# A two-block transformer on one core: row sums from natural-layout rows in the first stage, held order of its loads and splits, padding at the far end of SBUF

## The chip, the core and the metric

The kernel runs on one core of a Trainium2 chip. TensorE (PE) multiplies, VectorE (DVE) and ScalarE (ACT) work element by element, GpSimd (POOL) too, and SyncE (SP) issues the DMAs. All work from SBUF, 128 partitions wide; matmuls end in PSUM, which is used here as eight banks of 128x512 float32. The time is that of the whole program on the device, in microseconds, as the median of several runs. Three runs of the kernel before gave 1665.96, 1666.15 and 1666.22; the median is **1666.15 us**.

## The reference, cut to what matters

Two transformer blocks run one after the other on 512 tokens of 1024 features, float32 throughout. The change touches only how the first things of the first block are computed:

```
mem_n = mem * rsqrt(mean(mem*mem) + 1e-6) * g_mem       # 256 memory tokens
h     = x   * rsqrt(mean(x*x)     + 1e-6) * g_mix       # 512 tokens
k_m, v_m = split(mem_n @ w_mem_kv)                      # 1024 -> 2 x 512
q_m      = h @ w_in[:, 3072:3584]                       # 1024 -> 512
k = rmsnorm(k_m, per head of 128);  q = rmsnorm(q_m, per head of 128)
y_mem = softmax(q k^T / sqrt(128)) v                    # 4 heads
...   # moba attention, short convolution, gates, three branches, w_o, a feed-forward net
...   # second block: pooling branch, spatial gating branch, feed-forward net, gated embedding
```

The factor `rsqrt(mean)` is one number per token. So the kernel multiplies the weights with `mem * g_mem` and `x * g_mix`, not yet divided by the norm, and brings the factor in behind the product, where tokens are rows.

## The kernel before, in words

**Precision and weights.** Each float32 operand is split into a high part, rounded to the matmul's input type by ACT (`AF.Copy`), and a low part, what is left, by DVE (`split`, lines 183 to 190). A product is three matmuls: high by high, high by low, low by high. All weights come as one stream of 288 chunks of 128x1024 (512 KB), in the order in which they are used. Class `Weights` loads a chunk through SP (`load`, line 72), and splits it (`make`: ACT at line 92 writes `whi`, DVE at line 93 writes `wlo`). Raw, high and low chunks have three buffers each. `take` (line 97), called when the first piece of chunk c is used, loads up to chunk c+2 and splits up to chunk c+1. A load waits until the raw buffer is free, that is until the split of the chunk three before it is done; a copy to `whi` waits until TensorE is done with the chunk three before it.

**The first stage.** Nine matmuls on zeros run first (line 153). Then comes the projection of the memory to keys and values (lines 305 to 326), here called kv: eight steps k of 128 features each. A step splits the transposed memory's slice k (`mg{k}`), takes two pieces of 512 columns (one chunk), and does twelve matmuls into four banks `pk`. The memory comes transposed (`memT`, 128x8x256). Its squares are taken by ACT, summed over k by DVE (`Norm.add`, lines 263 to 278), and `per_token` (lines 280 to 288) transposes the sums on TensorE, adds them up on DVE and takes the inverse root (`rsqrt`, lines 239 to 255: ten dependent operations on DVE) to get `rmem`. The tokens come transposed as `xs` (128x8x512) in four loads placed in steps 1 to 4; each slice is split to `h{k}` (lines 341 to 344), and `xn` has its squares and its sum made by POOL (lines 338, 339, 345 and 346).

The keys are copied out of PSUM with the factor `rmem`, normed per head (`normed_rows`, lines 349 to 370) and transposed to `kmT`; the values become `vm`. The queries of the memory heads, here called qm, are 96 matmuls in `gemm_n_steps` (lines 211 to 221): eight steps k, each with four token tiles and three matmuls, two steps to a chunk. `FILL` says how many of these pieces come before the transposes of the keys and before `per_token` of `xn`, which gives `rx`. Then follow the other projections and attention.

**What sets the order.** The program is written in Python; a planner then orders the instructions of each engine by priority and by what its model of costs says is ready, keeps the dependences, and puts in the semaphores. So the order on a queue may differ from the order in the code. SP's queue works in order: a load that waits for a buffer holds up every load behind it.

**Where tiles lie.** Pools are stacked from both ends of SBUF. On the left are the constants, the weights, the operands `h`, the temporaries and most stages. Pools with `side="right"` are stacked from the far end, behind the pool "edge", a spacer of 96 bytes per partition: the memory attention's tiles, `y_conv`, `y_moba`, the pooled branch (`ypool`, `z`, `zs`, `pd`), the gated branch (`ysgu`) and `pT`. `space` (line 120) makes such spacers; others stand in the constants and in the small tiles.

Of the kernel before, what the change touches and what calls it, by code (L numbers as in the profile page):

```python
# [1 line left out]

# [17 lines left out]
KT = 8  # L20
# [6 lines left out]

WARM = 9

FILL = (9, 14, 8)  # L30

ORDER = (2, 3, 1, 0)

# [74 lines left out]
def build(ctx: ExitStack, tc: tile.TileContext, a: dict, out: bass.AP, dbg=None):  # L108
    nc = tc.nc
    mm = nc.tensor.matmul  # L110

    def pool(name, bufs=1, side=None, stack=None, space=None):
        kw = {} if space is None else {"space": space}
        if space is None:
            kw["reuse_waits"] = "tile"
            if side:
                kw["side"] = side
        return (stack or ctx).enter_context(tc.tile_pool(name=name, bufs=bufs, **kw))

# [6 lines left out]
    hpool = pool("operand")  # L126
    tmp = pool("tmp")
    small = pool("small", bufs=2)
    space(small, 64, "s")
    space(pool("edge", side="right"), 96, "e")  # L130
    PS = bass.MemoryType.PSUM
    acc = pool("acc", 5, space=PS)
    ps_s = pool("ps_s", 1, space=PS)
    ps_t = pool("ps_t", 1, space=PS)
    ps_o = pool("ps_o", 1, space=PS)
    W = Weights(nc, wpool, a["weights"])

    def dump(name, ap):
        if dbg is not None and name in dbg:
# [4 lines left out]
    r2 = ExitStack()  # L144
    st = pool("start", stack=r2)


    warm = st.tile([P, 512], BF16, name="warm")
    nc.vector.memset(warm, 0.0)
    nc.scalar.activation(st.tile([P, 1], BF16, name="table"), warm[:, :1], AF.Copy)  # L150
    wps = ps_o.tile([P, 512], F32, tag="po", name="warm")
    for _ in range(WARM):
        mm(wps, lhsT=warm[:, :P], rhs=warm, start=True, stop=True)
    vec = const.tile([P, NV], F32, name="vec")
    nc.sync.dma_start(vec[:, :16], a["vectors"][:, :16])
# [27 lines left out]
    def split(hi, lo, src, scale=None):  # L183

        if scale is None:
            nc.scalar.activation(hi, src, AF.Copy)
            nc.vector.tensor_tensor(lo, src, hi.bitcast(F32), ALU.subtract)
        else:
            nc.scalar.activation(hi, src, AF.Copy, scale=scale)
            nc.vector.scalar_tensor_tensor(lo, src, scale, hi.bitcast(F32), op0=ALU.mult, op1=ALU.subtract)  # L190
# [66 lines left out]
    class Norm:  # L257
# [5 lines left out]
        def add(self, x, by_pool=False):  # L263
            n = self.n

            def square(sq):
                if by_pool:
                    nc.gpsimd.tensor_tensor(sq, x, x, ALU.mult)
                else:
                    nc.scalar.activation(sq, x, AF.Square)  # L270

            if self.sum is None:
                self.sum = tmp.tile([P, 512], F32, tag="nsum", name=self.name + "s", bufs=1)[:, :n]
                square(self.sum)
            else:
                sq = temp(n, self.name + "q")
                square(sq)
                self.engine.tensor_tensor(self.sum, self.sum, sq, ALU.add)
# [23 lines left out]
    yp = pool("memat", stack=r1, side="right")  # L302


    pk = [bank() for _ in range(4)]
    mn = Norm("mem", M)
    for k in range(KT):
        ah, al = pair(st, f"mg{k}", f"mg{k}", 1, M)
        split(ah, al, memT[:, k, :], V("g_mem", k))
        if k == 0:  # L310
            W.make(1, 2)
        ws = [W.take("w_mem_kv", k * P, 512 * x, 512) for x in range(2)]
        mn.add(memT[:, k, :])
        if k == 1:
            nc.sync.dma_start(vec[:, 16:], a["vectors"][:, 16:])
        if 1 <= k < 5:
            q = 2 * k - 2
            nc.sync.dma_start(xs[:, q:q + 2, :], a["xT"][:, q:q + 2, :])
        for x in range(2):
            wh, wl = ws[x]  # L320
            for i in range(2):
                t = slice(i * P, (i + 1) * P)
                d = pk[2 * x + i]
                mm(d, lhsT=ah[:, t], rhs=wh, start=(k == 0), stop=False)
                mm(d, lhsT=al[:, t], rhs=wh, start=False, stop=False)
                mm(d, lhsT=ah[:, t], rhs=wl, start=False, stop=(k == KT - 1))

    qg = const.tile([P, 2], F32, name="qg")
    space(const, 1120, "c")
    nc.vector.tensor_scalar(qg[:, 0:1], V("moba_q_gain"), 64 ** -0.5, None, ALU.mult)  # L330
    nc.vector.tensor_scalar(qg[:, 1:2], V("memq_gain"), 128 ** -0.5, None, ALU.mult)
    rmem = mn.per_token()


    def operand(k):
        return pair(hpool, f"h{k}", f"h{k}", 1)
# [12 lines left out]
    def normed_rows(ps_list, nh, name, scales=None):  # L349
# [22 lines left out]
    vm = [pair(yp, f"vm{i}", f"vm{i}", 1) for i in range(2)]  # L372
    for i in range(2):
        split(*vm[i], pk[2 + i], rmem[:, i:i + 1])
    km_raw = [yp.tile([P, 512], F32, tag=f"kmr{i}", name=f"kmr{i}") for i in range(2)]
    normed_rows([(km_raw[i], pk[i]) for i in range(2)], 4, "km", rmem)
    pq = [bank() for _ in range(4)]
    qm_steps = gemm_n_steps(pq, h, "w_in", 3072)
    for _ in range(FILL[0]):
        next(qm_steps)  # L380
    kmT = [pair(yp, f"kmT{i}", f"kmT{i}", 1, 2 * M) for i in range(2)]
    for g in range(2):
        pt = bank(ps_t, "pt", "kmt")
        for hh in range(2):
# [12 lines left out]

# [577 lines left out]
```

## Time and profile before

| | |
|---|---|
| median of three runs | 1666.15 us |
| profiled execution: its own time | 1665.62 us |
| span of its instructions | 1663.9 us |
| granted TensorE clock, mean | 0.996 |
| TensorE busy | 1641.3 us (99%) |
| DVE, ACT, POOL busy | 956.5, 646.0 and 49.6 us |
| DMA | 161.37 MB, mean 97 GB/s |

The profile is of one execution, and its rows are measured from its first instruction. A row of the timeline has the start in us, the duration in us, the engine, the line, the operation, the output and inputs by name, and in square brackets how long the engine had been idle before it and what ended that. Matmuls are pipelined: two may overlap in such rows, so the distance between starts tells the pace. "PEld" is the loading of the stationary operand, which overlaps with matmuls. A row of groups gives the count, the sum and the mean in ns. A row of stretches gives for each engine the busy time and the count, then the granted clock (1.00 is full speed), the DMA engines' mean busy share and GB/s.

### The profile page before, as it was taken

Reading aid. Unit: us, or ns where it says so; the run is one execution under the profiler, and the core shown is the slowest. Engines: PE = TensorE matmul, PEld = TensorE weight load, DVE = VectorE, ACT = ScalarE, POOL = GpSimd, SP = SyncE. Lnnn points to the kernel's source line nnn. Section 1 sums busy time; section 2 is a strip of 40 time slices with the busy share of each in tenths; the row PEclk is TensorE's granted clock in tenths of the full one; section 3 lists DMA queues with packets and bytes.
Section 4 is the critical chain, followed back from the end, with each engine's and each line's share of the span. In section 5 each row is a group of like instructions: output and inputs, shape, how many; then the busy total and the mean of one; then the engine's idle time right before and its main releaser. Section 6 shows DMA issues by size and latency. Waiting matters only on the chain.

```text
span 1663.9 us, 18992 instructions
## 1 busy us (share of the span) xinstructions
PE 1641.3 (99%) x7553; PEld 1352.5 (81%) x7553; DVE 956.5 (57%) x1382; ACT 646.0 (39%) x927; POOL 49.6 (3%) x54
## 2 busy tenths in 40 slices
PE   6999999999999999999999999999999999999997
PEld 4788777888888888888888888888888888888887
DVE  8667776444556556563332943554467777753355
ACT  5455555222334333332224332333345444432253
POOL 5000000000000000000000300000000000000001
PEclk9999999999999999999999999999999999999999
DMA  5322222234232332323332333222333323323221
GB/s 208 114 77 76 65 62 65 89 101 147 94 101 89 102 100 91 102 92 99 101 117 90 98 102 98 92 89 89 101 102 101 98 93 101 95 95 102 92 99 51
DMA packets 46537, 161.37 MB, mean 97 GB/s; under 512 B 5232, under 2 KB 6640, under 8 KB 46448
## 3 DMA queue, kind: packets, MB, share of 16 engines
q1 hardware_dynamic: 46448, 160.16, 30.2%
q8 instruction: 59, 0.97, 0.2%
q14 instruction: 30, 0.25, 0.0%
HBM read 158.04 MB, written 2.10 MB: 96 GB/s over the span
## 4 chain that ended last, share of the span: by engine, by line
PE 96%; DVE 2%; ACT 1%; issue 0%; DMA 0%; SPq 0%; DVEq 0%; ACTq 0%
PE acc L206 27%; PE acc L207 27%; PE acc L208 27%; PE acc L218 2%; PE acc L220 2%; PE acc L219 2%; PE acc L857 1%; PE acc L856 1%; PE acc L855 1%; PE pat L544 1%; PE sg L791 0%; PE oa L559 0%; PE oa L560 0%; DMA memT<-in_memT 0%; DVE wlo L93 0%
## 5 line engine op out<-in xcount | busy, mean ns | idle before, releaser
L92 ACT ACTIVATE whi<-wraw 128x1024 fp32r<-128x1024 f32 (+1 forms) x289 | 305.5, 1057 | 586.1 <-PE acc L207 363.8
L93 DVE TENSOR_TENSOR wlo<-wraw,whi 128x1024 fp32r<-128x1024 f32 (+1 forms) x289 | 353.9, 1225 | 213.1 <-ACT whi L92 211.9
L206 PE MATMUL acc<-h0h,whi 128*128 128x512 f32 x156 | 62.2, 399 | 0.0
L206 PE MATMUL acc<-h7h,whi 128*128 128x512 f32 x156 | 61.3, 393 | 0.0
L207 PE MATMUL acc<-h0l,whi 128*128 128x512 f32 x156 | 61.2, 392 | 0.0
L206 PE MATMUL acc<-h2h,whi 128*128 128x512 f32 x156 | 61.1, 392 | 0.0
L206 PE MATMUL acc<-h6h,whi 128*128 128x512 f32 x156 | 61.1, 392 | 0.0
L206 PE MATMUL acc<-h5h,whi 128*128 128x512 f32 x156 | 61.1, 391 | 0.0
L206 PE MATMUL acc<-h1h,whi 128*128 128x512 f32 x156 | 61.0, 391 | 0.0
L206 PE MATMUL acc<-h3h,whi 128*128 128x512 f32 x156 | 61.0, 391 | 0.0
L208 PE MATMUL acc<-h0h,wlo 128*128 128x512 f32 x156 | 61.0, 391 | 0.0
L206 PE MATMUL acc<-h4h,whi 128*128 128x512 f32 x156 | 61.0, 391 | 0.0
L208 PE MATMUL acc<-h2h,wlo 128*128 128x512 f32 x156 | 60.9, 390 | 0.0
L208 PE MATMUL acc<-h5h,wlo 128*128 128x512 f32 x156 | 60.9, 390 | 0.0
L207 PE MATMUL acc<-h2l,whi 128*128 128x512 f32 x156 | 60.9, 390 | 0.0
L207 PE MATMUL acc<-h7l,whi 128*128 128x512 f32 x156 | 60.9, 390 | 0.0
L207 PE MATMUL acc<-h5l,whi 128*128 128x512 f32 x156 | 60.9, 390 | 0.0
L207 PE MATMUL acc<-h4l,whi 128*128 128x512 f32 x156 | 60.9, 390 | 0.0
L207 PE MATMUL acc<-h1l,whi 128*128 128x512 f32 x156 | 60.8, 390 | 0.0
L208 PE MATMUL acc<-h6h,wlo 128*128 128x512 f32 x156 | 60.8, 390 | 0.0
L207 PE MATMUL acc<-h6l,whi 128*128 128x512 f32 x156 | 60.8, 390 | 0.0
L208 PE MATMUL acc<-h7h,wlo 128*128 128x512 f32 x156 | 60.8, 390 | 0.0
(1271 smaller groups left out, 4079.8 us busy)
## 6 DMA issues: line engine op xcount, KB each, us to landing
wraw<-in_weights SPq DMA_DIRECT2D x287, 512.0 KB, 3.5
xs<-in_xT SPq DMA_DIRECT2D x4, 512.0 KB, 6.4
x<-in_xT SPq DMA_DIRECT2D x8, 256.0 KB, 5.9
out<-o SPq DMA_DIRECT2D x8, 256.0 KB, 2.1
wraw<-in_weights SPq DMA_DIRECT2D x2, 256.0 KB, 2.8
memT<-in_memT SPq DMA_DIRECT2D x1, 512.0 KB, 6.8
bb<-in_b_spatial SPq DMA_DIRECT2D x1, 512.0 KB, 4.8
ws<-in_w_spatialT SPq DMA_DIRECT2D x1, 512.0 KB, 5.6
```

Of the source, the lines that this page charges most:

```text
L92: nc.scalar.activation(hi[:, s], raw[:, s], AF.Copy)
L93: nc.vector.tensor_tensor(lo[:, s], raw[:, s], hi[:, s].bitcast(F32), ALU.subtract)
L206: mm(ps, lhsT=wh, rhs=ah, start=(k == 0), stop=False)
L207: mm(ps, lhsT=wh, rhs=al, start=False, stop=False)
L208: mm(ps, lhsT=wl, rhs=ah, start=False, stop=(k == n - 1))
L218: mm(ps, lhsT=ah[:, t], rhs=wh, start=(k == 0), stop=False)
L219: mm(ps, lhsT=ah[:, t], rhs=wl, start=False, stop=False)
L220: mm(ps, lhsT=al[:, t], rhs=wh, start=False, stop=(k == n - 1))
L544: nc.tensor.transpose(pt[:, i * P:(i + 1) * P], probs[s_][i][:, c0:c0 + P], ident)
L855: mm(pg, lhsT=wh, rhs=ah[:, t], start=(k == 0), stop=False)
L856: mm(pg, lhsT=wh, rhs=al[:, t], start=False, stop=False)
L857: mm(pg, lhsT=wl, rhs=ah[:, t], start=False, stop=(k == KT - 1))
```

## The change

The sums of squares of the memory and of the tokens are no longer made from the transposed slices. Both tensors are also given in natural layout (`"mem"`, `"x"`: tokens as rows), loaded in tiles of 128 rows of 4 KB (`load_rows`), and ACT squares each tile in place and sums along the row in the same instruction (`row_sums`). The result has one number per token at once, without sums over k, transposes and a reduction. POOL and DVE no longer take part in these sums.

A context manager `as_written` adds an order between successive instructions of SP, ACT and DVE, so that from the first instruction to the last x split the planner keeps the order of the code. That order is written out: the memory's first half goes through ACT's DMA queue, in two loads; the splits of the memory run two steps ahead of their use; x loads, row loads, x splits and row sums each have a step. The kv accumulators use two of the five `acc` banks and the banks `ps_s` and `ps_o`, so that three `acc` banks are free when qm begins. The transposed memory is now in two tiles of 4 KB per partition which share four buffers with the row tiles.

The spacer "edge" has 224 bytes instead of 96, a spacer of 128 bytes is added in the pooled branch's pool behind `ypool`, and the tile "table" in the first stage's pool has 256 bytes instead of 2.

```diff
-FILL = (9, 14, 8)
+FILL = (3, 8)
...
-    space(pool("edge", side="right"), 96, "e")
+    space(pool("edge", side="right"), 224, "e")
...
+    @contextmanager
+    def as_written(*engines):
+        traced = nc.cur_bb.bb.instructions
+        n = len(traced)
+        yield
+        last = {}
+        for i in traced[n:]:
+            if i.engine in engines:
+                if i.engine in last:
+                    tc.add_manual_dep(i, last[i.engine].name, mybir.DependencyInfo(
+                        mybir.DependencyClass.NoSync, mybir.DependencyReason.DATA), reason="order")
+                last[i.engine] = i
...
+    order = as_written(mybir.EngineType.SP, mybir.EngineType.Activation, mybir.EngineType.DVE)
+    order.__enter__()
...
-    nc.scalar.activation(st.tile([P, 1], BF16, name="table"), warm[:, :1], AF.Copy)
...
+    memT = [st.tile([P, D], F32, tag="rows", name=f"memT{i}", bufs=4).rearrange("p (k m) -> p k m", m=M) for i in range(2)]
+    nc.scalar.dma_start(memT[0][:, 0:1, :], a["memT"][:, 0:1, :])
+    nc.scalar.dma_start(memT[0][:, 1:4, :], a["memT"][:, 1:4, :])
+    nc.scalar.activation(st.tile([P, P], BF16, name="table")[:, :1], warm[:, :1], AF.Copy)
     nc.sync.dma_start(vec[:, :16], a["vectors"][:, :16])
-    memT = st.tile([P, KT, M], F32, name="memT")
-    nc.sync.dma_start(memT[:, 0:1, :], a["memT"][:, 0:1, :])
     W.load(1, 2)
-    nc.sync.dma_start(memT[:, 1:2, :], a["memT"][:, 1:2, :])
     W.load(2)
-    nc.sync.dma_start(memT[:, 2:4, :], a["memT"][:, 2:4, :])
-    nc.sync.dma_start(memT[:, 4:8, :], a["memT"][:, 4:8, :])
+    nc.sync.dma_start(memT[1], a["memT"][:, 4:8, :])
     W.load(3)
...
+    def load_rows(name, i):
+        t = st.tile([P, D], F32, tag="rows", name=f"{name}{i}", bufs=4)
+        nc.sync.dma_start(t, a[name][i * P:(i + 1) * P, :])
+        rows.append(t)
+
+    def row_sums(sums, i):
+        t = rows.pop(0)
+        nc.scalar.activation(t, t, AF.Square, accum_out=sums[:, i:i + 1])
...
-    pk = [bank() for _ in range(4)]
-    mn = Norm("mem", M)
+    pk = [bank(), bank(), bank(ps_s, "ps"), bank(ps_o, "po")]
+    ssm = small.tile([P, 4], F32, tag="nss", name="ssm")
+    ssx = small.tile([P, 4], F32, tag="nss", name="ssx")
...
+    make_mg(0)
+    W.make(1, 2)
+    make_mg(1)
     for k in range(KT):
...
         ws = [W.take("w_mem_kv", k * P, 512 * x, 512) for x in range(2)]
-        mn.add(memT[:, k, :])
+        make_mg(k + 2)
         if k == 1:
+            load_x(0)
+        elif k == 3:
+            load_rows("mem", 0)
+        elif k == 4:
+            load_rows("mem", 1)
+        elif k == 5:
+            make_h(0)
+        elif k == 6:
+            load_x(2)
+            row_sums(ssm, 0)
+            make_h(1)
+        elif k == 7:
+            row_sums(ssm, 1)
+            rmem = rsqrt(ssm[:, :2], 2, 1.0 / D, "n")
             nc.sync.dma_start(vec[:, 16:], a["vectors"][:, 16:])
-        if 1 <= k < 5:
-            q = 2 * k - 2
-            nc.sync.dma_start(xs[:, q:q + 2, :], a["xT"][:, q:q + 2, :])
+            load_x(4)
+            load_x(6)
+            make_h(2)
...
-    rmem = mn.per_token()
...
-    xn.engine = nc.gpsimd
-    h = []
-    for k in range(KT):
-        hk = operand(k)
-        split(*hk, xs[:, k, :], V("g_mix", k))
-        h.append(hk)
-    for k in range(KT):
-        xn.add(xs[:, k, :], by_pool=True)
...
-    for _ in range(FILL[0]):
-        next(qm_steps)
...
-    for _ in range(FILL[1]):
-        next(qm_steps)
-    rx = xn.per_token()
+    for k in range(KT):
+        if k == FILL[0]:
+            transpose_km()
+        if k >= 4:
+            row_sums(ssx, k - 4)
+        for _ in range(4):
+            next(qm_steps)
+        if k == 0:
+            for i in range(2):
+                split(*vm[i], pk[2 + i], rmem[:, i:i + 1])
+        elif k == 1:
+            for i in range(2):
+                load_rows("x", i)
+        elif k == 2:
+            for i in range(2, 4):
+                load_rows("x", i)
+        if k + 3 < KT:
+            make_h(k + 3)
+    order.__exit__(None, None, None)
     run(qm_steps)
+    xn.r = rx = rsqrt(ssx, 4, 1.0 / D, "n")
...
     PAD = 32
+    space(pp, 128, "p")
...
+        "x": np.ascontiguousarray(g["x"][0]),
+        "mem": np.ascontiguousarray(g["mem"][0]),
```

More of the change, by code (lines that the diff above doesn't have):

```diff
@@ L1 @@
-from contextlib import ExitStack
+from contextlib import ExitStack, contextmanager
 import concourse.bass as bass
@@ L154, in build @@
     vec = const.tile([P, NV], F32, name="vec")
+    memT = [st.tile([P, D], F32, tag="rows", name=f"memT{i}", bufs=4).rearrange("p (k m) -> p k m", m=M) for i in range(2)]
+    nc.scalar.dma_start(memT[0][:, 0:1, :], a["memT"][:, 0:1, :])
+    nc.scalar.dma_start(memT[0][:, 1:4, :], a["memT"][:, 1:4, :])
+    nc.scalar.activation(st.tile([P, P], BF16, name="table")[:, :1], warm[:, :1], AF.Copy)
     nc.sync.dma_start(vec[:, :16], a["vectors"][:, :16])
-    memT = st.tile([P, KT, M], F32, name="memT")
-    nc.sync.dma_start(memT[:, 0:1, :], a["memT"][:, 0:1, :])
     W.load(1, 2)
-    nc.sync.dma_start(memT[:, 1:2, :], a["memT"][:, 1:2, :])
     W.load(2)
-    nc.sync.dma_start(memT[:, 2:4, :], a["memT"][:, 2:4, :])
-    nc.sync.dma_start(memT[:, 4:8, :], a["memT"][:, 4:8, :])
+    nc.sync.dma_start(memT[1], a["memT"][:, 4:8, :])
     W.load(3)
     xs = st.tile([P, KT, S], F32, name="xs")
+    rows = []
+    def load_rows(name, i):
[5 more added lines that the diff above has]
+        nc.scalar.activation(t, t, AF.Square, accum_out=sums[:, i:i + 1])
     def V(name, j=0):
@@ L261, in __init__, with add @@
             self.name, self.n, self.sum, self.engine = name, n, None, nc.vector
-        def add(self, x, by_pool=False):
+        def add(self, x):
             n = self.n
             def square(sq):
[L267 to L270, printed above, removed]
+                nc.scalar.activation(sq, x, AF.Square)
             if self.sum is None:
@@ L302, in build, with operand, make_h, load_x @@
     yp = pool("memat", stack=r1, side="right")
-    pk = [bank() for _ in range(4)]
-    mn = Norm("mem", M)
+    def operand(k):
+        return pair(hpool, f"h{k}", f"h{k}", 1)
+    h = [operand(k) for k in range(KT)]
+    def make_h(k):
+        split(*h[k], xs[:, k, :], V("g_mix", k))
+    def load_x(k):
+        nc.sync.dma_start(xs[:, k:k + 2, :], a["xT"][:, k:k + 2, :])
+    pk = [bank(), bank(), bank(ps_s, "ps"), bank(ps_o, "po")]
+    ssm = small.tile([P, 4], F32, tag="nss", name="ssm")
+    ssx = small.tile([P, 4], F32, tag="nss", name="ssx")
+    mg = [pair(st, f"mg{k}", f"mg{k}", 1, M) for k in range(KT)]
+    def make_mg(k):
+        if k < KT:
+            split(*mg[k], memT[k // 4][:, k % 4, :], V("g_mem", k))
+    make_mg(0)
+    W.make(1, 2)
+    make_mg(1)
     for k in range(KT):
[L308 to L311, printed above, removed]
+        ah, al = mg[k]
         ws = [W.take("w_mem_kv", k * P, 512 * x, 512) for x in range(2)]
-        mn.add(memT[:, k, :])
+        make_mg(k + 2)
         if k == 1:
+            load_x(0)
[12 more added lines that the diff above has]
+            rmem = rsqrt(ssm[:, :2], 2, 1.0 / D, "n")
             nc.sync.dma_start(vec[:, 16:], a["vectors"][:, 16:])
-        if 1 <= k < 5:
-            q = 2 * k - 2
-            nc.sync.dma_start(xs[:, q:q + 2, :], a["xT"][:, q:q + 2, :])
+            load_x(4)
+            load_x(6)
+            make_h(2)
         for x in range(2):
@@ L329, in build @@
     space(const, 1120, "c")
-    nc.vector.tensor_scalar(qg[:, 0:1], V("moba_q_gain"), 64 ** -0.5, None, ALU.mult)
-    nc.vector.tensor_scalar(qg[:, 1:2], V("memq_gain"), 128 ** -0.5, None, ALU.mult)
-    rmem = mn.per_token()
-    def operand(k):
-        return pair(hpool, f"h{k}", f"h{k}", 1)
-    xn = Norm("x")
-    xn.engine = nc.gpsimd
-    h = []
-    for k in range(KT):
-        hk = operand(k)
-        split(*hk, xs[:, k, :], V("g_mix", k))
-        h.append(hk)
-    for k in range(KT):
-        xn.add(xs[:, k, :], by_pool=True)
+    xn = Norm("x")
     def normed_rows(ps_list, nh, name, scales=None):
@@ L370, in normed_rows, with transpose_km @@
         return raws
-    vm = [pair(yp, f"vm{i}", f"vm{i}", 1) for i in range(2)]
-    for i in range(2):
-        split(*vm[i], pk[2 + i], rmem[:, i:i + 1])
     km_raw = [yp.tile([P, 512], F32, tag=f"kmr{i}", name=f"kmr{i}") for i in range(2)]
     normed_rows([(km_raw[i], pk[i]) for i in range(2)], 4, "km", rmem)
+    vm = [pair(yp, f"vm{i}", f"vm{i}", 1) for i in range(2)]
+    nc.vector.tensor_scalar(qg[:, 0:1], V("moba_q_gain"), 64 ** -0.5, None, ALU.mult)
+    nc.vector.tensor_scalar(qg[:, 1:2], V("memq_gain"), 128 ** -0.5, None, ALU.mult)
+    kmT = [pair(yp, f"kmT{i}", f"kmT{i}", 1, 2 * M) for i in range(2)]
+    def transpose_km():
+        for g in range(2):
+            pt = bank(ps_t, "pt", "kmt")
+            for hh in range(2):
+                for i in range(2):
+                    c = (2 * g + hh) * P
+                    nc.tensor.transpose(pt[:, hh * M + i * P: hh * M + (i + 1) * P], km_raw[i][:, c:c + P], ident)
+            split(*kmT[g], pt, V("memk_gain"))
     pq = [bank() for _ in range(4)]
     qm_steps = gemm_n_steps(pq, h, "w_in", 3072)
-    for _ in range(FILL[0]):
-        next(qm_steps)
[L381 to L384, printed above, removed]
-            for i in range(2):
-                c = (2 * g + hh) * P
-                nc.tensor.transpose(pt[:, hh * M + i * P: hh * M + (i + 1) * P], km_raw[i][:, c:c + P], ident)
-        split(*kmT[g], pt, V("memk_gain"))
-    for _ in range(FILL[1]):
-        next(qm_steps)
-    rx = xn.per_token()
+    for k in range(KT):
[6 more added lines that the diff above has]
+        if k == 0:
+            for i in range(2):
+                split(*vm[i], pk[2 + i], rmem[:, i:i + 1])
[8 more added lines that the diff above has]
+    order.__exit__(None, None, None)
     run(qm_steps)
+    xn.r = rx = rsqrt(ssx, 4, 1.0 / D, "n")
     qm_raw = [yp.tile([P, 512], F32, tag=f"qmr{i}", name=f"qmr{i}") for i in range(4)]
@@ L466, in build @@
     filler = qkv_steps()
-    for _ in range(FILL[2]):
+    for _ in range(FILL[1]):
         next(filler)
```

## The prediction, made before the result

> **What bounds the kernel now.** I read the page's busy times first, then who waits on TensorE, then busy time by stretch, then the order of instructions in the first 70 us.
>
> ```profile
> PE 1641.3 (99%) x7553; PEld 1352.5 (81%) x7553; DVE 956.5 (57%) x1382; ACT 646.0 (39%) x927; POOL 49.6 (3%) x54
> PE 96%; DVE 2%; ACT 1%; issue 0%; DMA 0%; SPq 0%; DVEq 0%; ACTq 0%
> ```
> ```profile
> PE acc L326 <- DVE wlo L93: 8.2, 3, 3.7
> PE acc L324 <- ACT whi L92: 3.2, 3, 1.4
> ```
> TensorE carries the span, and nearly all that it waits for is in two groups of lines 324 to 326, the projection of the memory tokens at the very start (I call it kv; it has eight steps of twelve matmuls). The stretches confirm it:
>
> ```profile
> 5.00:24.00 19.00, 15.10 (x60) 11.02 (x61) 16.71 (x28) 15.73 (x28) 3.78 (x3) 1.00 0.93 338
> 24.00:32.20 8.20, 4.66 (x22) 3.41 (x19) 8.17 (x9) 3.45 (x4) 7.58 (x6) 0.94 0.37 117
> 32.20:45.00 12.80, 9.12 (x21) 6.66 (x22) 12.09 (x13) 2.04 (x4) 11.74 (x11) 0.64 0.27 86
> 400.00:800.00 400.00, 400.00 (x1768) 330.69 (x1767) 221.85 (x280) 146.65 (x180) 0.00 (x0) 1.00 0.30 97
> ```
> The columns are PE, its weight loads, DVE, ACT and POOL, then clock, DMA share and GB/s. From 24 to 45 us DVE and POOL are busy all the time, ACT is nearly idle and DMA is at a third; then the clock falls to 0.64. Later TensorE has no gap at all. So the first 45 us can give, and elsewhere only the pace of the matmuls. The starts of matmuls that mark the steps:
>
> ```profile
> 5.17 0.50 PE L324 MATMUL acc<-whi,mg0h 128*128 128x512 f32 x1 [0.48 <-ACT whi L92]
> 9.54 0.50 PE L324 MATMUL acc<-whi,mg1h 128*128 128x512 f32 x1 [1.30 <-ACT whi L92]
> 13.98 0.50 PE L324 MATMUL acc<-whi,mg2h 128*128 128x512 f32 x1 [1.37 <-ACT whi L92]
> 22.34 0.74 PE L326 MATMUL acc<-wlo,mg4h 128*128 128x512 f32 x2 [1.00 <-DVE wlo L93]
> 24.53 0.39 PE L325 MATMUL acc<-whi,mg5l 128*128 128x512 f32 x1
> 27.09 0.40 PE L324 MATMUL acc<-whi,mg6h 128*128 128x512 f32 x1
> 32.23 1.65 PE L326 MATMUL acc<-wlo,mg6h 128*128 128x512 f32 x3 [3.57 <-DVE wlo L93]
> 34.10 0.63 PE L325 MATMUL acc<-whi,mg6l 128*128 128x512 f32 x1
> 34.53 0.63 PE L326 MATMUL acc<-wlo,mg6h 128*128 128x512 f32 x1
> 41.37 1.55 PE L326 MATMUL acc<-wlo,mg7h 128*128 128x512 f32 x3 [3.65 <-DVE wlo L93]
> 43.99 0.63 PE L218 MATMUL acc<-whi,h0h 128*128 128x512 f32 x1
> 67.96 0.39 PE L218 MATMUL acc<-whi,h0h 128*128 128x512 f32 x1
> ```
> Undisturbed, eleven matmuls take 27.09 - 24.53 = 2.56 us, 0.2325 us each, so a step takes 2.79 us. At the halved clock each takes 0.43 us. From the third step (13.98) to the end of kv (43.99) pass 30.0 us for 72 matmuls that need 72 x 0.2325 = 16.7. The excess of 13.3 us is the waits of 1.00, 3.57 and 3.65, some 18 matmuls at the low clock (18 x 0.195 = 3.5 us), two transposes and short gaps. The second projection (qm, 96 matmuls) runs from 43.99 to 67.96.
>
> **Why DVE is late.** Groups by line and shape in the first 70 us, then one tile's POOL group:
>
> ```profile
> L93 DVE TENSOR_TENSOR wlo<-wraw,whi 128x1024 fp32r<-128x1024 f32 x13 | 16.5, 1272 | 2.5 <-ACT whi L92 2.5
> L190 DVE SCALAR_TENSOR_TENSOR h5l<-xs,vec,h5h 128x512 fp32r<-128x512 f32 x1 | 1.9, 1857 | 0.0
> L190 DVE SCALAR_TENSOR_TENSOR h6l<-xs,vec,h6h 128x512 fp32r<-128x512 f32 x1 | 0.7, 739 | 0.0
> L248 DVE SCALAR_TENSOR_TENSOR nb<-nb,nv 128x2 f32<-128x2 f32 x1 | 1.2, 1230 | 0.0
> L248 DVE SCALAR_TENSOR_TENSOR nb<-nb,nv 128x4 f32<-128x4 f32 x1 | 0.2, 166 | 0.0
> ```
> ```profile
> L278 POOL TENSOR_TENSOR xs<-xs,xq x7: 1262/1738/2213, 27.1 to 40.2; 128x512 f32<-128x512 f32 x7
> ```
> The same ten-operation inverse root takes 0.17 us an operation when POOL is idle and about 1.2 us beside POOL's adds; a split takes 0.74 against 1.86 us. It and the x splits stand ahead of the weight splits that TensorE waits for.
>
> **The change, part by part.** *Removed:* POOL's eight squares and seven adds, ACT's eight squares and DVE's seven adds over the transposed memory rows, six transposes and two reductions. With POOL silent, DVE's operations go back to 0.17 and 0.74 us.
>
> *Added:* six row loads of 512 KB (3.1 MB) and six ACT squares over 128x1024 with an accumulated sum. The trace has no such square; the nearest rows are
>
> ```profile
> 8.43 1.06 ACT L92 ACTIVATE whi<-wraw 128x1024 fp32r<-128x1024 f32 x1 [0.43 <-DMA wraw<-in_weights]
> 12.88 1.04 ACT L92 ACTIVATE whi<-wraw 128x1024 fp32r<-128x1024 f32 x1
> ```
> ```profile
> L724 ACT ACTIVATE vq<-sv x8: 626/628/641, 891.2 to 912.1; 128x512 f32<-128x512 f32 x8
> L724 ACT ACTIVATION_READ_ACCUMULATOR vq<-sv x8: 185/197/210, 891.8 to 912.6; 128x1 f32 x8
> ```
> Between 1.06 + 0.20 and 2 x 0.63 + 0.20, so 1.3 us; two fall in kv, four in qm. ACT then needs at most 1.06 (weight) + 1.3 + 0.71 (x split) = 3.1 us in the two steps that have all three and 1.6 to 2.3 in the others, against 2.79; it works a step ahead of TensorE, so I count nothing. If that lead were gone, 0.3 us a step.
>
> *Loads at the start.* Memory rows 0 to 3 (512 KB) go on ACT's queue beside SP's, weight chunk 1 behind chunk 0 on SP's. What the DMA moved:
>
> ```profile
> 0.00:5.00 5.00, 3.44 (x9) 1.13 (x9) 0.76 (x2) 2.74 (x5) 1.09 (x8) 1.00 0.44 144
> 5.00:8.40 3.40, 3.07 (x12) 2.18 (x12) 2.03 (x4) 1.56 (x4) 0.00 (x0) 1.00 0.85 273
> 8.40:12.90 4.50, 3.07 (x12) 2.17 (x12) 3.67 (x10) 4.32 (x11) 0.00 (x0) 1.00 1.01 397
> ```
> By 8.4 us 0.72 + 0.93 = 1.65 MB had moved, and chunk 1, with 1.32 MB up to it, had just landed (ACT's 8.43). Now 1.58 MB stand up to it: it lands between 8.2 (if those 1.65 MB are moved in the new order) and 8.4 + 0.26/0.397 = 9.1. A rise of 9.54 - 8.43 = 1.11 us to the matmul gives step 1 at 9.3 to 10.2; I take 9.7. [...] Up to chunk 2 the bytes are those of before; there it had landed by 12.88 (ACT took it without waiting). TensorE is free at 9.7 + 2.79 = 12.5, and the bound from ACT's row is 12.88 + 1.11 = 14.0: I take 13.2 for step 2.
>
> *From there on.* The queue works off 512 KB in 1.3 us at 397 GB/s. With chunk 2 landed at 12.1 and the order of the changed code (chunk 3, x 0-1, chunks 4 and 5, memory rows 0, chunk 6, memory rows 1, chunk 7), the low part being ready 1.1 + 1.2 us after the landing:
>
> ```
> chunk          3     4     5     6     7
> lands       13.4  16.0  17.3  19.9  22.5
> low ready   15.7  18.3  19.6  22.2  24.8
> step begins 16.0  18.8  21.6  24.4  27.2
> ```
> A chunk's load waits on SP until the split of the chunk three before it is done (15.7 for chunk 6, 18.3 for chunk 7: before their turn in the queue), and the row and x loads stand behind that wait; x 0-1 is wanted at step 5, the memory rows at 6 and 7, all landed by 21.2. So no wait is left, though chunks 3 and 4 have only 0.3 and 0.5 us: six steps of 2.79, kv ends at 13.2 + 16.7 = 29.9 instead of 43.99, **-14.1**. The two issues on ACT (some 0.4 us each) and the table load behind them lie ahead of ACT's first copy, which waits for the landing anyway.
>
> *qm.* Three of its matmuls lose the low clock (0.6) and four transposes go (0.36 by the row below): **-0.9**. The held DVE order puts the memory keys' norm ahead of weight chunk 9's split. Chunk 8's copy needs the buffer that TensorE leaves at 24.4; row sum and split end at 26.7, the inverse root (ten times 0.2) at 28.7, ACT's two copies and two squares of the keys (four times 0.65) at 31.3, the last reduction (0.7) at 32.0, the second root at 34.0, two products (0.7) at 35.4, chunk 9's low part at 36.6. The third qm step wants it at 29.9 + 5.4 + 0.2 = 35.5, so 1.1 us late. The order on TensorE is free, and eight matmuls with the high part (1.9 us) can go first: 0 to 1.1, I take **+0.5**. Behind that split stand the splits of h3 to h7, each with 0.5 us or more to spare.
>
> ```profile
> 61.34 0.60 PE L284 MATMUL xp<-ident,xs 128*128 128x128 f32 x4
> 61.70 0.49 PE L218 MATMUL acc<-whi,h5h 128*128 128x512 f32 x1
> ```
>
> *The padding.* Pools at the far end of SBUF are stacked behind a spacer of 96 bytes, now 224. Matmuls that read them, and one family that does not suffer:
>
> ```profile
> 1117.72 0.40 PE L206 MATMUL acc<-ys0h,whi 128*128 128x512 f32 x1
> 1123.31 0.39 PE L206 MATMUL acc<-h0h,whi 128*128 128x512 f32 x1
> ```
> ```profile
> 1024.17 0.39 PE L206 MATMUL acc<-yp0h,whi 128*128 128x512 f32 x1
> 1029.61 0.39 PE L206 MATMUL acc<-h0h,whi 128*128 128x512 f32 x1
> ```
> 24 matmuls on ys take 5.59 us (233 ns), 24 on yp 5.44 (227 ns), although both lie at the far end. All tiles there have 2048 bytes, except five of 2176 (8.5 x 256) between yp and the rest of its pool: yp's start differs from ys's by 128 modulo 256. The new spacer adds 128 to all, and 128 more inside yp's pool leave yp in its class and bring its neighbours into it. By the loops 96 (y_conv) + 96 (y_moba) + 192 (ys) + 48 (pooled) + 48 (pT) = 480 matmuls read such tiles: 480 x 6 ns, **-2.9** if the class decides, 0 if not, and +192 x 6 ns = +1.2 if yp falls into the slow class instead. The widened "table" tile moves kv's stationary tiles by 224 bytes in the same way: 0 to 96 x 5.5 ns = 0.5, I take **-0.3**.
>
> **The sum.** -14.1 - 0.9 + 0.5 - 2.9 - 0.3 = -17.7 us. The profiled execution took 1665.62 (span 1663.9 and 1.7 around it), so 1647.9; the median of the runs lies 0.5 above it: **1648.4 us**.
>
> **Rivals.** *The padding does nothing:* for it, no row here shows a tile before and after a move; against it, yp. 1651.3. *The clock falls again:* after 3.57 idle it did, after 1.30 and 1.37 it did not. Step 1 is preceded by some 1.7 idle; a later landing makes it 2.2. A fall costs 3.4 to 6.8 us at 0.43 instead of 0.23 a matmul, 1.6 to 3.1 us: 1650.8. [...] *The held order makes new waits:* a late row load stops ACT, and every weight copy behind it; 2 to 4 us over kv and qm, 1651.4. *DMA binds kv:* 6.8 MB stand up to chunk 7; it must land by 26, so under 6.8 / 24 = 283 GB/s it would bind; 338 is the mean seen. At 260 GB/s 2.2 us: 1650.6. *The order is not held* and the planner's stays: POOL's silence remains, waits as at 9.54 and 22.34 too: 1650.
>
> *The other side, slower:* SP's queue turns into a lock step: each chunk waits for the split three before it, with row loads ahead of it in the queue. It decides when three steps no longer cover landing + 1.06 + 1.22.
>
> ```profile
> DMA to landing us min/median/max: 2.7/4.2/7.6
> ```
> At the longest landing that is 9.9 / 3 = 3.3 us a step, 0.5 above 2.79, or 6 us over twelve chunks: 1654. To be slower by 0.2% each chunk would have to lose (17.7 + 3.3) / 12 = 1.75 us, a landing of 11.3 us throughout: 1670. Against it: the longest of before is 7.6.
>
> **How the numbers follow.** Forecast 0.56; padding without effect 0.12; new waits 0.12; clock 0.08; DMA 0.05; order not held 0.03; slower 0.03; about the same 0.01. The low end takes the early landing of chunks 1 and 2 (kv's end at 29.2, or 28 if chunk 1 comes near 7), no late split, and 0.5 for the table tile: 1645. The high end takes the padding's 2.9 and one of the other rivals: 1653.5. About 0.2%, 3.3 us, can be told from no change: faster 0.96, same 0.01, slower 0.03.
>
> **What would show it.** No POOL adds before 45 us; the memory's inverse root near 0.17 us an operation; the first h0h matmul of qm near 30 us; granted clock 1.00 from 5 to 45; idle ahead of mg1h near 1.7 and ahead of mg2h under 1; ys steps of 24 matmuls in 5.44 us, yp unchanged. Wrong if kv ends after 34, if a wait on a load or on row sums appears between steps 3 and 8, or if ys keeps 5.59.

## The result and the profile after

The changed kernel takes 1650.44 us (median of 4 runs, 1650.08 to 1650.85) against 1666.18 us of the kernel before on the same chip (1665.96 to 1666.57): a ratio of 0.9905, 95% interval [0.9888, 0.9923], or 15.7 us less. The profiled execution took 1650.08 us, its span is 1648.4. I had predicted a time of 1648.4, that is 17.7 less.

Busy times on the page after:

```profile
PE 1634.2 (99%) x7547; PEld 1350.7 (82%) x7547; DVE 941.0 (57%) x1373; ACT 648.4 (39%) x931; POOL 28.2 (2%) x39
```
POOL lost 21.4 us of work, and TensorE is still busy for 99% of the span. Two of the stretches shown before (columns PE, its weight loads, DVE, ACT, POOL, clock, DMA share, GB/s):

```profile
24.00:32.20 8.20, 8.20 (x38) 6.79 (x37) 6.24 (x16) 6.19 (x10) 0.00 (x0) 1.00 0.98 364
32.20:45.00 12.80, 11.10 (x50) 8.52 (x49) 10.71 (x24) 7.19 (x11) 0.00 (x0) 1.00 0.72 269
```
POOL is silent, TensorE has no gap from 24 to 32.2 (4.66 of 8.20 before), and the clock stays at 1.00 where it was 0.64. From 32.2 to 45, though, 1.7 us are still missing. The starts of matmuls that mark the steps:

```profile
6.68 2.42 PE L382 MATMUL acc<-whi,mg0h 128*128 128x512 f32 x4 [1.41 <-ACT whi L93]
11.25 0.39 PE L382 MATMUL acc<-whi,mg1h 128*128 128x512 f32 x1
13.97 0.39 PE L382 MATMUL acc<-whi,mg2h 128*128 128x512 f32 x1
30.29 0.39 PE L246 MATMUL acc<-whi,h0h 128*128 128x512 f32 x1
35.73 1.07 PE L246 MATMUL acc<-whi,h2h 128*128 128x512 f32 x4
38.10 0.55 PE L427 MATMUL kmt<-ident,kmr 128*128 128x128 f32 x3 [0.21 <-DVE kmr L411]
39.35 0.50 PE L247 MATMUL acc<-wlo,h2h 128*128 128x512 f32 x1 [0.71 <-DVE wlo L94]
55.56 0.39 PE L246 MATMUL acc<-whi,h0h 128*128 128x512 f32 x1
```
So the span divides as follows; the rows of before stand in the prediction.

| stretch | before | after | measured | predicted |
|---|---|---|---|---|
| up to the end of kv | 43.99 | 30.29 | -13.7 | -14.4 (table tile included) |
| qm | 23.97 | 25.27 | **+1.3** | -0.4 |
| the rest | 1595.94 | 1592.84 | -3.1 | -2.9 |
| span | 1663.9 | 1648.4 | -15.5 | -17.7 |

The kv steps from the third on have no wait: 72 matmuls in 30.29 - 13.97 = 16.32 us, 226.7 ns each. The error lies in qm (1.7 us) and in kv's first two steps (0.7). In qm four matmuls of the third step go at 35.73, and then TensorE stands still for the key transposes and for the low part of weight chunk 9. Why that part is late, on ACT, on SP and on DVE:

```profile
27.11 1.06 ACT L93 ACTIVATE whi<-wraw 128x1024 fp32r<-128x1024 f32 x1 [0.42 <-DMA wraw<-in_weights]
```
```profile
21.05 0.33 SPq L73 DMA_DIRECT2D wraw<-in_weights  x1
```
```profile
29.34 0.16 DVE L272 TENSOR_SCALAR nv<-ssm 128x2 f32<-128x2 f32 x1
36.75 1.29 DVE L411 TENSOR_TENSOR kmr<-kmr,kmy 128x512 f32<-128x512 f32 x2
38.08 1.22 DVE L94 TENSOR_TENSOR wlo<-wraw,whi 128x1024 fp32r<-128x1024 f32 x1
```
SP issues the load of chunk 8 at 21.05, when the split of chunk 5, three before it, is done (at 21.03). ACT copies the chunk at 27.11, when it lands, and takes the second row sum behind it; then come the inverse root (0.16 us an operation, ten of them from 29.34 to 31.28), the keys' norm, and only then chunk 9's split, done at 39.30. Matmuls on ys, at last, take 5.44 us for 24 instead of 5.59:

```profile
1103.26 0.39 PE L234 MATMUL acc<-ys0h,whi 128*128 128x512 f32 x1
1108.70 0.39 PE L234 MATMUL acc<-h0h,whi 128*128 128x512 f32 x1
```

### The profile page after: what moved, and what is told of

Its sections match the earlier page's. It is cut to its first block, busy times and chain, and to the rows that moved or that the text cites. A ratio compares the mean times of both kernels' runs of the same rounds, so it can differ in the third digit from the quotient of the medians.

```text
span 1648.4 us, 18944 instructions
## 1 busy us (share of the span) xinstructions
PE 1634.2 (99%) x7547; PEld 1350.7 (82%) x7547; DVE 941.0 (57%) x1373; ACT 648.4 (39%) x931; POOL 28.2 (2%) x39
## 4 chain that ended last, share of the span: by engine, by line
PE 98%; DVE 1%; ACT 0%; DMA 0%; issue 0%; DVEq 0%; SPq 0%; ACTq 0%
PE acc L234 27%; PE acc L235 27%; PE acc L236 27%; PE acc L247 3%; PE acc L248 3%; PE acc L246 3%; PE acc L917 1%; PE acc L916 1%; PE acc L915 1%; PE pat L603 1%; PE acc L382 0%; PE sg L851 0%; PE acc L383 0%; PE oa L618 0%; PE acc L384 0%; PE oa L619 0%
```

## The experiments

Times of different groups of runs are compared by their distance from the kernel before in the same group, since that kernel itself went from 1666.2 to 1666.6 us.

**The padding alone (p1_pad_only).** The kernel before, with

```
-    space(pool("edge", side="right"), 96, "e")
+    space(pool("edge", side="right"), 224, "e")
+    space(pp, 128, "p")
```


> The kernel before with the padding of the change alone: spacer 224 instead of 96 bytes, and 128 bytes inside the pool of yp; the first stage and the table tile are untouched. If the start address modulo 256 decides, the 480 matmuls on yc, yo, ys, pd and pT fall from 233 to 227 ns and the time by 2.9 to 3.1 us (ratio 0.9982), while kv keeps 232.5 ns a matmul and the first 68 us stay as they are. If the faster matmuls that the changed kernel shows there come from somewhere else (the first stage, other tiles), it is 0 here.

1663.47 us against 1666.59, ratio 0.9982 [0.9972, 0.9991], so 3.1 us less. Starts of 24 matmuls on ys and of what follows, in this kernel:

```profile
1106.06 0.39 PE L206 MATMUL acc<-ys0h,whi 128*128 128x512 f32 x1
1111.50 0.39 PE L206 MATMUL acc<-h0h,whi 128*128 128x512 f32 x1
```
They take 5.44 us. What comes behind qm takes 1592.9 us here, 3.1 less than in the kernel before. The padding brings its 3.1 us by itself; 12.6 of the change's 15.7 are left for the first stage.

**Which addresses are slow (e128, e160, e192t).** The changed kernel without the 128 bytes in yp's pool and with another spacer; e192t has the narrow table tile too:

```
-    space(pool("edge", side="right"), 224, "e")
+    space(pool("edge", side="right"), 128, "e")      # 160, 192
-    space(pp, 128, "p")
...
-    nc.scalar.activation(st.tile([P, P], BF16, name="table")[:, :1], warm[:, :1], AF.Copy)
+    nc.scalar.activation(st.tile([P, 1], BF16, name="table"), warm[:, :1], AF.Copy)
```


> The changed kernel with a spacer of 128 bytes and none inside the pool of yp. Counted back from the far end modulo 256, yc, yo, ys, pd and pT start at 128 and yp at 0. Known: 160 is slow (233 ns; the kernel before), 32 is fast (227; both kernels, and the changed one for ys). If one half of the 256 bytes is slow, 128 to 255, ys and its like are at 233 and yp at 227: 2.9 us above the changed kernel. If 160 is a single bad place, both are at 227 and the time is the changed kernel's.

> As e128, with a spacer of 160 bytes: yc, yo, ys, pd and pT start at 96 and yp at 224. If the half from 128 on is slow: ys at 227, yp at 233 (192 matmuls, 1.2 us above the changed kernel). If 160 is a single bad place: both at 227.

> As e128, with a spacer of 192 bytes: yc, yo, ys, pd and pT start at 64 and yp at 192; and the table tile has its old width of one column, so that the memory's split tiles of kv start 224 to 254 bytes lower, as in the kernel before. If the half from 128 on is slow: ys at 227, yp at 233, 1.2 us. If the table tile's width is what brought kv from 232.5 to 227 ns a matmul, kv goes back to 232.5 and takes 0.5 us more; if the new order of the first stage did that, it stays at 227.

One execution each: 1657.23, 1654.68 and 1654.88 us, 4 to 7 us above the changed kernel, though 1.0 to 1.9 us of that is a later end of kv in these executions. What counts is the pace of the tiles that were moved. In e128:

```profile
1003.53 0.40 PE L234 MATMUL acc<-yp0h,whi 128*128 128x512 f32 x1
1009.13 0.39 PE L234 MATMUL acc<-h0h,whi 128*128 128x512 f32 x1
...
1108.76 0.40 PE L234 MATMUL acc<-ys0h,whi 128*128 128x512 f32 x1
1114.37 0.40 PE L234 MATMUL acc<-h0h,whi 128*128 128x512 f32 x1
```
In e160:

```profile
1001.85 0.39 PE L234 MATMUL acc<-yp0h,whi 128*128 128x512 f32 x1
1007.45 0.39 PE L234 MATMUL acc<-h0h,whi 128*128 128x512 f32 x1
...
1106.96 0.40 PE L234 MATMUL acc<-ys0h,whi 128*128 128x512 f32 x1
1112.47 0.40 PE L234 MATMUL acc<-h0h,whi 128*128 128x512 f32 x1
```
In e192t, with the kv steps from the third on ahead of them:

```profile
14.45 0.40 PE L382 MATMUL acc<-whi,mg2h 128*128 128x512 f32 x1
31.25 0.39 PE L246 MATMUL acc<-whi,h0h 128*128 128x512 f32 x1
...
1001.28 0.40 PE L234 MATMUL acc<-yp0h,whi 128*128 128x512 f32 x1
1006.90 0.40 PE L234 MATMUL acc<-h0h,whi 128*128 128x512 f32 x1
...
1106.49 0.40 PE L234 MATMUL acc<-ys0h,whi 128*128 128x512 f32 x1
1112.10 0.40 PE L234 MATMUL acc<-h0h,whi 128*128 128x512 f32 x1
```
Both guesses fall: it is neither one half nor a single place that is slow, but every start except one. My counting from the far end had its zero 32 bytes off; by the addresses that the pools give the tiles when the kernels are built (ys0h at 180,096 before, which is 703.5 x 256, and at 179,968 = 703 x 256 after) the table reads:

| start modulo 256 | 0 | 32 | 64 | 96 | 128 | 160 | 192 | 224 |
|---|---|---|---|---|---|---|---|---|
| tile, kernel | ys, after | ys, e192t | ys, e160 | ys, e128 | ys, before | yp, e192t | yp, e160 | yp, e128 |
| 24 matmuls, us | 5.44 | 5.61 | 5.51 | 5.61 | 5.59 | 5.62 | 5.60 | 5.60 |

Of these only the tile that starts at a multiple of 256 bytes is read in 5.44 us; the others take 5.51 to 5.62. The same shows in kv: with the narrow table tile the memory's split tiles start 32 bytes past a multiple, and 72 matmuls take 31.25 - 14.45 = 16.80 us, 233 ns each, against 16.32 with the wide one. Those tiles are the stationary operand in kv, while ys and yp are the moving one, so both kinds were slower off a multiple. For the stationary one no other offset was tried, and no other width of matmul for either.

**POOL's work put back (g1_pool_adds, g2_pool_memset).** The changed kernel with work for POOL whose result nobody uses; in the second kernel the loop holds `nc.gpsimd.memset(junk, 0.0)`, forty times:

```
             load_x(0)
+            junk = st.tile([P, S], F32, name="junk")
+            nc.gpsimd.tensor_tensor(junk, xs[:, 0, :], xs[:, 1, :], ALU.mult)
+            for _ in range(14):
+                nc.gpsimd.tensor_tensor(junk, junk, xs[:, 1, :], ALU.add)
```


> The changed kernel with fifteen operations of POOL added that nobody waits for: one product of two x slices (128x512), then fourteen adds of a slice onto the result, from about 14 us on; they stand for the squares and adds that were removed. If POOL's work slows DVE beside it, as read from the profile of before, operations of the memory's inverse root that fall beside them take about 1.2 instead of 0.17 us and the splits of x 1.9 instead of 0.74; the inverse root, ahead of the keys' norm and of chunk 9's split on DVE, then ends some 5 to 10 us later, and the time is 1655 to 1662. If the gain came from the new order of loads and splits alone, POOL may work as it likes: 1650 to 1651.

> As the run with POOL's adds, but after the first product POOL only writes: forty memsets of the same 128x512 tile, some 0.5 us each, from about 14 to 35 us. If any work of POOL slows DVE, the small operations take about 1.2 us as there and the time is 1655 to 1662; if only POOL operations that read two operands do, it is 1650 to 1651.

One execution each: 1660.55 us with the adds, 1650.87 with the memsets. With the adds, POOL's group by tile, DVE's weight splits from 14 to 42 us, DVE in order of time, and the start of qm on TensorE:

```profile
L363 POOL TENSOR_TENSOR junk<-junk,xs x14: 1262/1476/2162, 16.9 to 39.8; 128x512 f32<-128x512 f32 x14
```
```profile
L94 DVE TENSOR_TENSOR wlo<-wraw,whi 128x1024 fp32r<-128x1024 f32 x6 | 12.7, 2123 | 0.8 <-ACT whi L93 0.8
```
```profile
35.82 1.25 DVE L272 TENSOR_SCALAR nv<-ssm 128x2 f32<-128x2 f32 x1
37.10 0.17 DVE L274 TENSOR_SCALAR ny<-nv 128x2 int32<-128x2 int32 x1
37.30 1.13 DVE L275 TENSOR_TENSOR nb<-ny 128x2 f32<-128x2 f32 x1
```
```profile
36.04 0.39 PE L246 MATMUL acc<-whi,h0h 128*128 128x512 f32 x1
```
And with the memsets:

```profile
L363 POOL MEMSET junk<- x40: 524/526/532, 16.1 to 38.8; 128x512 f32 x40
```
```profile
28.91 0.56 DVE L272 TENSOR_SCALAR nv<-ssm 128x2 f32<-128x2 f32 x1
29.50 0.55 DVE L274 TENSOR_SCALAR ny<-nv 128x2 int32<-128x2 int32 x1
30.08 0.16 DVE L275 TENSOR_TENSOR nb<-ny 128x2 f32<-128x2 f32 x1
```
```profile
L94 DVE TENSOR_TENSOR wlo<-wraw,whi 128x1024 fp32r<-128x1024 f32 x7 | 8.6, 1224 | 3.6 <-ACT whi L93 2.6 <-PE acc L387 0.9
```
POOL works from 16 to 40 us in both. Beside its adds five of the six weight splits take 2.3 instead of 1.22 us (the mean of 2.12 has one that began ahead of POOL), and every second small operation takes about 1.1 instead of 0.17; ten microseconds of the gain are gone. kv ends at 36.04 instead of 30.29, and qm takes 4.6 us longer. In the kernel before kv ended at 43.99; what the shorter way to the sums and the other order of loads and splits add to the adds' part there was not separated. Beside memsets the splits keep 1.22 us, and only some operations with a single input tile take longer: here the first two of the inverse root, 0.56 and 0.55 us instead of 0.16 and 0.17 (one memset takes 0.53), while its third (line 280) keeps 0.17 us. So it isn't POOL's work as such that slows DVE operations with two inputs: a split takes 2.3 us beside the adds, which read two tiles, and 1.22 beside the memsets, which only write (an operation of POOL that reads a single tile was not tried).

**The held order taken away (o1_no_hold).**

```
-    order.__enter__()
...
-    order.__exit__(None, None, None)
```


> The changed kernel without the added dependences that hold SP, ACT and DVE to the order as written in the first stage; the planner orders them. Theory: POOL's silence carries the gain and the planner's order only brings some waits on weight splits back, +1 to +3 us against the changed kernel (1651.5 to 1653.5), with the memory's inverse root still at 0.17 us an operation. Rival: the held order carries the gain, and without it kv ends after 38 us, +8 us or more. A third: the held order is what puts the keys' norm ahead of weight chunk 9's split, and without it qm loses its waits: -1 to -2 us.

1648.48 us (1648.02 to 1649.43) against 1666.59: ratio 0.9891 [0.9876, 0.9905], 18.1 us less than before, where the changed kernel has 15.7. The runs of the two don't overlap; their intervals do, from 0.9888 to 0.9905. By its median it is the fastest kernel of this study. The theory (waits on weight splits come back, 1 to 3 us more) missed, and the third guess came true. TensorE, and DVE where it splits chunk 9:

```profile
30.89 0.39 PE L245 MATMUL acc<-whi,h0h 128*128 128x512 f32 x1
...
53.79 0.39 PE L245 MATMUL acc<-whi,h0h 128*128 128x512 f32 x1
```
```profile
32.43 1.23 DVE L94 TENSOR_TENSOR wlo<-wraw,whi 128x1024 fp32r<-128x1024 f32 x1 [0.57 <-ACT whi L93]
```
The planner takes chunk 9's split at 32.43, ahead of the keys' norm, not at 38.08 behind it. qm takes 22.90 us instead of 25.27, and kv ends only 0.6 us later. The order as written gains nothing here and costs about 2 us.

**Chunk 9's split first, the order still held (k1_split_first).**

```
+    W.make(10)
     normed_rows([(km_raw[i], pk[i]) for i in range(2)], 4, "km", rmem)
...
-FILL = (3, 8)
+FILL = (4, 8)
```


> The changed kernel, order still held, with chunk 9's split written ahead of the keys' norm and the key transposes one qm step later (first number of FILL 4 instead of 3). Theory: chunk 9's low part, put behind the inverse root and not behind the keys' norm, is ready at 32.5 to 33 us, before its step at 35.7, and the waits of 0.8, 0.2 and 0.7 us on the keys' norm and on the split go: 1.7 to 2.2 us less than the changed kernel, 1648.2 to 1648.7 where that is 1650.4. Rival: something else in qm (the load of chunk 10, the splits of x) is late next and takes it back, 0 to 0.5 us less.

1648.83 us (1648.38 to 1650.24) against 1666.35, ratio 0.9895 [0.9882, 0.9909]: 17.5 us less than before, 1.8 more than the change brings, as the theory had it. The slowest of its four runs lies among those of the changed kernel, and the intervals overlap, so the trace carries more weight here than the time. In qm one wait is left:

```profile
32.84 0.50 PE L246 MATMUL acc<-whi,h0h 128*128 128x512 f32 x1 [0.32 <-ACT kmr L402]
```
The waits on the keys' norm and on the split are gone, and a small one on the keys' copy (a bank that qm wants) stands in their place. So the cause of qm's loss was where the held order has the split and the transposes of the keys; the edit moves both, and their parts were not separated.

**The start (l1_mem_late, c1_both, o2_no_hold_late, s1_split_issue).** In l1 rows 1 to 3 of the memory go on SP's queue; c1 is l1 with the edit of k1, o2 is l1 without the held order. In s1 (on k1) they stay on ACT's queue but are issued behind ACT's first copy:

```
-    nc.scalar.dma_start(memT[0][:, 1:4, :], a["memT"][:, 1:4, :])
...
     W.load(1, 2)
+    nc.sync.dma_start(memT[0][:, 1:4, :], a["memT"][:, 1:4, :])      # l1, c1, o2
     W.load(2)
...
     make_mg(0)
+    nc.scalar.dma_start(memT[0][:, 1:4, :], a["memT"][:, 1:4, :])    # s1
     W.make(1, 2)
```


> The changed kernel with memory rows 1 to 3 (384 KB) taken off ACT's queue and put on SP's queue behind weight chunk 0, so that chunk 0's first half has less beside it. The start should come back: first kv matmul at 5.2 to 5.5 instead of 6.68, step 1 at 9.6 instead of 11.25, kv's end 1.2 to 1.7 us earlier. Theory: qm does not begin its third step any earlier, since the chain that ends in chunk 9's low part (landing of chunk 8, row sum of memory rows 1, inverse root, keys' norm, split) hangs on landings and not on kv's end; the stall grows by what kv gains and the time falls by 0 to 0.3 us. Rival: start and qm add up, and the time falls by 1.2 to 1.7 us.

> Both edits: memory rows 1 to 3 on SP's queue behind chunk 0, and chunk 9's split ahead of the keys' norm. Theory: now kv's earlier end counts: 1.7 to 2.2 us for the split and 1.0 to 1.5 for the start, 2.7 to 3.7 less than the changed kernel. Rival: the landing of chunk 8 (27.0 us, its low part 2.3 us later) keeps qm from beginning before 29.5, and only the split's part remains, 2.0 to 2.5 less.

> The changed kernel without the held order (it gained 2 us in an earlier run) and with memory rows 1 to 3 on SP's queue behind chunk 0. There the first kv matmul came at 7.36 us and its first step ran at the low clock; kv then had no wait up to its end at 30.89. Theory: first matmul at 5.2 to 5.6, the clock of step 0 stays high as in the kernel before, kv ends at 28.5 to 29.2 and nothing later gives it back: 1.5 to 2.2 us less than without the held order alone, 1646.3 to 1647 where that is 1648.5. Rival: kv is then bound by the landings of chunks 5 to 8 and gains under 0.5 us.

> The kernel of k1_split_first (chunk 9's split ahead of the keys' norm), with memory rows 1 to 3 still loaded from ACT's queue, but issued behind ACT's first copy (about 4.5 us) instead of at 1.2 us: weight chunk 0 has less beside it, and two queues still carry the loads. Theory: first kv matmul at 5.2 to 5.5, the clock stays high through step 0, chunk 1 lands by 8.7 as before and step 1 begins at 9.5 to 9.8 instead of 11.2; kv ends 1.0 to 1.7 us earlier than in k1_split_first, 1647.1 to 1647.8 where that is 1648.8. Rival: the landings of chunks 3 to 7 bind kv once it runs earlier (step 3 waited 0.53 us for chunk 3 there), and it gains 0 to 0.5.

The four theories missed: none of these kernels is faster than what it was to improve. l1 and s1 are slower in every run; c1 and o2 only by their medians, and their runs overlap with those of k1 and o1.

| kernel | us | of before | ratio and interval | less than before |
|---|---|---|---|---|
| l1_mem_late | 1651.62 | 1666.35 | 0.9912 [0.9898, 0.9925] | 14.7 (the change: 15.7) |
| c1_both | 1649.87 | 1666.35 | 0.9901 [0.9887, 0.9914] | 16.5 (k1: 17.5) |
| o2_no_hold_late | 1649.50 | 1666.35 | 0.9899 [0.9885, 0.9912] | 16.9 (o1: 18.1) |
| s1_split_issue | 1653.49 | 1666.46 | 0.9919 [0.9905, 0.9932] | 13.0 (k1: 17.5) |

In l1 the first matmul does come early, and the second step doesn't. TensorE, then ACT:

```profile
5.37 1.42 PE L382 MATMUL acc<-whi,mg0h 128*128 128x512 f32 x4 [0.53 <-ACT whi L93]
11.13 0.79 PE L382 MATMUL acc<-whi,mg1h 128*128 128x512 f32 x1 [2.51 <-ACT whi L93]
```
```profile
10.02 1.06 ACT L93 ACTIVATE whi<-wraw 128x1024 fp32r<-128x1024 f32 x1 [0.70 <-DMA wraw<-in_weights]
```
Chunk 1 lands 1.6 us later than in the changed kernel (copied at 10.02 instead of 8.42), with the same bytes ahead of it. What the DMA moves from 5 to 7 us, first in the changed kernel, then in l1:

```profile
5.00:7.00 2.00, 0.59 (x2) 0.32 (x2) 0.34 (x1) 0.63 (x1) 0.00 (x0) 1.00 1.00 336
```
```profile
5.00:7.00 2.00, 1.63 (x6) 1.12 (x7) 1.38 (x2) 0.95 (x2) 0.00 (x0) 1.00 0.84 187
```
With these rows on SP's queue the DMA moves 187 GB/s in these two microseconds instead of 336. In s1 the piece issued later on ACT's queue:

```profile
4.26 0.33 ACTq L351 DMA_DIRECT2D memT<-in_memT  x1
12.62 0.51 ACT L216 ACTIVATE mg1h<-memT,vec 128x256 fp32r<-128x256 f32 x1 [5.79 <-DMA memT<-in_memT]
```
It lands 8.3 us after its issue. All of its 384 KB (0.39 MB) move from 8 to 12.3 us, beside what stands on SP's queue, and nothing of it before. The queues' packets, MB and share in these 4.3 us (q1 is SP's, q10 ACT's):

```profile
q1 hardware_dynamic: 349, 1.27, 78.2%
q10 hardware_dynamic: 144, 0.39, 22.7%
```
The change's own early issue on ACT's queue is, by the medians, the best of the three places tried. The theory of l1 (qm hangs on landings, so nothing gained at the start arrives) was not put to the test, since the start was not gained.

## Why the prediction was right, and where it was off

- **POOL's silence, -14.1 us up to kv's end: right in size.** Measured -13.7. DVE's small operations went to 0.16 us and the splits of x to 0.75. With POOL's adds put back 10 us of the gain are lost again, but only 5.8 of them up to kv's end and 4.6 in qm; that POOL's silence alone is worth all of kv's 13.7 is not shown.
- **"Step 1 at 9.7, step 2 at 13.2": late, 0.8 us.** Chunk 1's copy ended at 9.48, within what I had worked out, but TensorE was not free: I had silently kept the first matmul of before (5.17), though 384 KB more now run beside chunk 0. It came at 6.68, and its step took 11.25 - 6.68 = 4.57 us instead of 2.72. Two of its first four matmuls need the second half of chunk 0, whose copy ends at 7.82; the next three start at 8.89 and are followed at 10.10, 0.40 us each, which is close to the 0.43 of the low clock. The 1.00 of the stretches doesn't speak against it, since the trace's first record of the clock, 1.00, stands at 10.0 us. So the slow pace of the rival "the clock falls again" came about a step earlier than I had it; whether it was the clock, no record shows. The same code took 3.6 us in k1_split_first, where three matmuls from 8.39 to 9.08 are 0.23 us apart; there kv ended at 30.31 all the same, after a wait of 0.53 us for chunk 3's low part. No run shows the "chunk 1 comes near 7" of the low end: ACT's copy of that chunk began at 8.42 here and at 8.32 (g2) at the earliest.
- **Six undisturbed steps, and the order of the loads: right.** No wait from 13.97 to 30.29. The chunks came later than in my table (chunk 7 copied at 23.97, when I had it landed at 22.5), but ahead of their steps.
- **qm, "+0.5": mis-sized, it cost 2.2.** The step that failed is "chunk 8's copy needs the buffer that TensorE leaves at 24.4". I never worked out chunk 8's landing; the copy waited for it until 27.11, since SP could issue the load only at 21.05, behind the split of chunk 5. From there the chain took 39.30 - 27.11 = 12.2 us, just what I had added up (36.6 - 24.4). And of the eight matmuls that were to go first only four did, because the planner put the key transposes, which wait for the same chain, ahead of the rest. Two runs remove these waits and gain 1.8 and 2.4 us.
- **The padding, -2.9: right, 3.1 by itself.** My ground (ys and yp differ by 128 modulo 256) was true, but I took it for two classes. There is one good start and seven bad ones, which is why padding one pool and pushing yp elsewhere would have cost, by my estimate, some 1.2 us (192 matmuls on yp, 6 ns each).
- **The table tile, -0.3: 0.5.** By e192t's one execution the 72 matmuls from the third step on gain 6.7 ns each, 0.5 us.
- **The rivals.** Of "the held order makes new waits" the price was right (2 us) and the place wrong: no row load stopped ACT; a norm stood ahead of a split. "The order is not held" I had priced at 1650; it came out at 1648.5, better than the order held. A bound by DMA did not come about. SP's lock step held up no step of kv, but it is what made chunk 8 late: landing, copy and split of that chunk (6.1 + 1.06 + 1.22 = 8.3 us) took as long as three steps (8.2).

## What to carry to other kernels

Look for operations of DVE that take many times their usual duration (here 1.1 to 1.25 us instead of 0.17), and for what POOL reads at that moment; here some 23 us of POOL's adds, off the path, cost 10 us on it. When an order is fixed by hand, follow it past the stage it was written for: the first split wanted by the next stage must not stand behind a chain that nobody wants yet. Start the operands of TensorE at multiples of 256 bytes (seen here for float32 pieces and 512 columns: 5.44 us for 24 matmuls against 5.51 to 5.62), and compare the pace of matmuls by operand to find those that don't.

## What the runs showed of the hardware that was not expected

- With an operand that starts off a multiple of 256 bytes a matmul of 512 columns took 3 to 7.5 ns more than 227 ns. For the moving one this was seen at each of the seven 32-byte offsets (5.51 to 5.62 us for 24 against 5.44), for the stationary one at the only offset tried, 32 (233 ns).
- Beside POOL's adds every second small DVE operation kept its usual duration in g1: 1.25, 0.17, 1.13, 0.16, 1.11 and 0.16 us in a row from 35.82. In the kernel before three in a row from 37.00 took 0.96, 0.97 and 1.18 us.
- A load on a second queue need not be served at once: the piece that ACT issued at 4.26 us in s1 moved nothing before 8 us, and was there at 12.6. From 8 to 12.3 us its 0.39 MB moved beside 1.27 of SP's; the four microseconds of waiting before that stay open. In l1 one queue instead of two made chunk 1 land 1.6 us later, four times the 0.4 us of an issue. Why the DMA moved only 187 GB/s there from 5 to 7 us was not found: the 384 KB of memory rows in line with the weights may do it, or the single queue.
- kv's first step takes 3.6 to 5.9 us, from a first matmul between 6.5 and 7.1 us, in seven executions whose code is the same up to there (the changed kernel, k1, g1, g2 and the three with other spacers). The pace of the matmuls explains much of it: three of them take 0.23 us each in k1 (8.39 to 9.08), 0.40 in the changed kernel (8.89 to 10.10) and 0.43 in e128 (9.51 to 10.79). The nine matmuls on zeros had ended 1.34, 1.41 and 1.79 us ahead of the first one there, so having them did not make sure of the 0.23. What sets the clock was not found. In the kernel before it was 0.50 from 31.27 to 38.09 us and from 41.51 to 44.92; in the 3.41 us ahead of these stretches TensorE was busy for 0.80 and 0.13 us. It stayed at 1.00 from 7.37 to 17.61 us, with TensorE busy for 2.11, 2.03 and 3.35 us of each third.
